# A column roll of 8192 x 8192 floats: the last eighth of the long row pieces issued as DMAs of one row per engine, two in flight on each ring

## The chip, the cores and the metric

The kernel runs on one core of a Trainium2 chip. The metric is the device time in microseconds, as the median of several runs. A core has five instruction streams (TensorE or PE, VectorE or DVE, ScalarE or ACT, GpSimd or POOL, SyncE or SP) and 16 DMA engines. SP, ACT and POOL issue DMAs, and each has a queue of its own to them: in the profile q1 is SP's, q10 is ACT's, q0 is POOL's. The queues of SP and ACT are called rings here. The other core of the pair is idle.

## The reference

```python
def setup_inputs():
    return {"x": np.random.randn(8192, 8192).astype(np.float32), "shift": 100}

def reference(x, shift):
    return np.roll(x, shift, axis=1)
```

Every row moves right by 100 columns, and its last 100 columns come to its front. Nothing is computed: 268 MB are read from the chip's memory and 268 MB are written.

## The kernel before

A row of the output is cut at column `a` = 128, the first multiple of 128 at or after the shift `s` = 100; `g` = a - s = 28.

**The long pieces.** Columns 128 to 8191 of the output are columns 28 to 8091 of the input: 8064 floats or 32,256 bytes of each row, copied from memory to memory without passing through the core. Rows are seen as `"(c e j) w -> j e c w"` with e = 16 and j = 4: row = 64 c + 4 e + j. There are 128 blocks `c` of 64 rows. A DMA (L37) takes one `j`, all 16 values of `e`, and 32 blocks, so its shape is [16, 32, 8064], 16.1 MB, with `e` outermost: each of the 16 DMA engines gets one `e` and copies 32 rows. The loop runs over four `c` ranges and over `j`; `engines[j % 2]` sends even `j` to SP and odd `j` to ACT, so each ring gets eight such DMAs.

**The heads.** The first 128 columns of each row are 512 bytes. POOL reads them into on-chip tiles and writes them again. A row's head is made of the last 100 columns of that row and its first 28 columns. Since the end of one row lies in memory just ahead of the start of the next, three of four heads are read with one piece of 128 floats that runs across the row boundary (`lead`, L67). These pieces are one row apart in what they hold, so DVE copies them into place in the tile `h` (L69 and L72). The fourth is read in two pieces (L68, L71). There are two stages `k` of 4096 rows each, hence ten loads; then eight stores (L76) write the heads.

**Order.** Nothing orders the long pieces against the heads, since their bytes are apart. The framework gives each DMA one of eight semaphores for the hardware queues (shared by SP and ACT) and one of eight for POOL's queue, and a DMA waits until its semaphore's previous user is done. So the fifth to eighth DMA of a ring each wait for the DMA four before them (L37), and POOL's ninth and tenth load (L68 and L71 of the second stage) wait for its first and second. At the end SP waits for all of them.

Of the kernel before, what the change touches and what calls it, by code (L numbers as in the profile page):

```python
# [1 line left out]

# [4 lines left out]


@with_exitstack
def kernel(  # L10
    ctx: ExitStack,
    tc: tile.TileContext,
    x: bass.AP,
    shift: int,
    out: bass.AP,
):
    nc = tc.nc
    n_rows, n_cols = x.shape
    s = shift % n_cols
    a = -(-s // 128) * 128  # L20
    g = a - s
    P = nc.NUM_PARTITIONS
    engines = [nc.sync, nc.scalar]
    n_chunks = 16
    rows = n_rows // n_chunks

    xm = x.rearrange("(c e j) w -> j e c w", e=16, j=4)  # L30
    om = out.rearrange("(c e j) w -> j e c w", e=16, j=4)
    depth = n_rows // 64 // 4
    for c in range(4):
        for j in range(4):
            if a < n_cols:
                cs = slice(c * depth, (c + 1) * depth)
                engines[j % 2].dma_start(out=om[j, :, cs, a:], in_=xm[j, :, cs, g:n_cols - s])  # L37
    if a == 0:
        return


    if a > 512:
        for i in range(n_chunks):
            r = slice(i * rows, (i + 1) * rows)
            nc.gpsimd.dma_start(out=out[r, :s], in_=x[r, n_cols - s:])
            if g > 0:
                nc.gpsimd.dma_start(out=out[r, s:a], in_=x[r, :g])
        return

    Q, J = 4, 8
    n_st = n_rows // (P * Q * J)
    reads = ctx.enter_context(tc.tile_pool(name="reads", bufs=n_st))
    heads = ctx.enter_context(tc.tile_pool(name="heads", bufs=n_st))
    xt = x.rearrange("(k p j q) c -> k q p j c", q=Q, j=J, p=P)
    ot = out.rearrange("(k p j q) c -> k q p j c", q=Q, j=J, p=P)
    tiles = []  # L60
    for k in range(n_st):
        t = reads.tile([P, Q - 1, J, a], x.dtype)
        h = heads.tile([P, Q, J, a], x.dtype)
        for q in range(1, Q):
            lead = bass.AP(tensor=x.tensor, offset=(k * P * J * Q + q) * n_cols - s,
                           ap=[[J * Q * n_cols, P], [Q * n_cols, J], [1, a]])
            nc.gpsimd.dma_start(out=t[:, q - 1], in_=lead)  # L67
        nc.gpsimd.dma_start(out=h[:, Q - 1, :, :s], in_=xt[k, Q - 1, :, :, n_cols - s:])  # L68
        nc.vector.tensor_copy(h[:, :Q - 1, :, :s], t[:, :, :, :s])  # L69
        if g > 0:  # L70
            nc.gpsimd.dma_start(out=h[:, 0, :, s:], in_=xt[k, 0, :, :, :g])  # L71
            nc.vector.tensor_copy(h[:, 1:, :, s:], t[:, :, :, s:])  # L72
        tiles.append(h)
    for k, h in enumerate(tiles):
        for q in range(Q):
            nc.gpsimd.dma_start(out=ot[k, q, :, :, :a], in_=h[:, q])  # L76


# [1 line left out]
_INS = ['x', 'shift']  # L80
_OUTS = [((8192, 8192), 'float32')]

_NUMBERS = {'shift': 100}


# [26 lines left out]
```

## Time and profile before

| what | value |
|---|---|
| median of 8 runs | 831.7 us (827.97 to 832.84) |
| the profiled execution, its own time | 832.84 us |
| its span in the profile | 831.1 us |
| bytes moved by the DMA engines | 272.63 MB in 10784 packets |
| mean rate | 328 GB/s |
| long DMAs on SP and on ACT | 8 each of 16128 KB, median 407.7 and 406.9 us from issue to landing |
| POOL's loads | 10, up to 512 KB, medians 121 to 156 us to landing |
| POOL's stores | 8 of 512 KB, median 187.3 us to landing |
| DVE busy | 3.7 us in 4 copies |

How to read the profile: the span is the time from the first to the last instruction that the profiler saw, and the device time has some 1.7 us around it. The DMA row of part 2 has the mean busy share of the 16 DMA engines in 40 slices of about 20.8 us, in tenths. Part 3 gives each queue's packets, megabytes, and the time of its packets as a share of the time of 16 engines. A DMA-issuing instruction of SP or ACT isn't counted as busy; in the timeline and in the waits its engine is called SPq or ACTq. When windows of time are asked for, each line has the window, its length, busy time and instruction count of DVE and POOL, the clock of PE, the DMA busy share and the rate. A packet is counted in the window in which it starts, so a very short window can show a share above 1.

### The profile page before, as it was taken

The numbers are of one execution on the slowest core, as the hardware profiler recorded it, in microseconds if no ns is written. First come the engines' busy times: TensorE is split into PE (matmuls) and PEld (weight loads), VectorE is DVE, ScalarE is ACT, GpSimd is POOL, SyncE is SP. The second block draws the span as 40 slices with busy tenths as digits, with TensorE's granted clock in tenths as the row PEclk, the third lists the DMA queues.
The fourth block names the chain that finished last, engine by engine and source line by source line (L and its number), as shares of the span: only waits on it lengthen the run. The fifth ranks groups of instructions, "written<-read, shape, count | busy, mean of one in ns | idle before, by whom it ended". The sixth has DMA issues, their size and how long they took to land. (4 is left out here: it accounts for less than half of the span.)

```text
span 831.1 us, 93 instructions
## 1 busy us (share of the span) xinstructions
DVE 3.7 (0%) x4; POOL 16.1 (2%) x22
## 2 busy tenths in 40 slices
DVE  0000000000000000000000000000000000000000
POOL 3000001000010000000000000000000000000000
DMA  9999999999999999999999999999999999999996
GB/s 301 319 342 323 318 335 333 330 339 329 337 328 341 332 338 340 334 341 329 345 325 336 337 332 320 332 324 329 326 323 331 324 329 323 320 334 326 328 332 258
DMA packets 10784, 272.63 MB, mean 328 GB/s; under 512 B 544, under 2 KB 544, under 8 KB 2592
## 3 DMA queue, kind: packets, MB, share of 16 engines
q1 hardware_dynamic: 4224, 132.12, 47.0%
q10 hardware_dynamic: 4224, 132.12, 46.9%
q0 software_dynamic: 2336, 8.39, 4.7%
HBM read 268.44 MB, written 268.44 MB: 646 GB/s over the span
## 5 line engine op out<-in xcount | busy, mean ns | idle before, releaser
L76 POOL DMA_DIRECT2D out_dram<-h x8 | 6.9, 955 | 175.0 <-DMA h<-in_x_dram 148.3
L67 POOL DMA_DIRECT2D t<-in_x_dram x6 | 5.4, 911 | 0.8 <-PEq L107 0.8
L69 DVE COPY h<-t 128x2400 f32<-128x2400 f32 x2 | 2.8, 1411 | 213.6 <-DMA t<-in_x_dram 213.6
L71 POOL DMA_DIRECT2D h<-in_x_dram x2 | 1.8, 882 | 29.3 <-DMA t<-in_x_dram 29.3
L68 POOL DMA_DIRECT2D h<-in_x_dram x2 | 1.8, 883 | 27.0 <-DMA t<-in_x_dram 27.0
L72 DVE COPY h<-t 128x672 f32<-128x672 f32 x2 | 1.0, 504 | 0.0
L93 POOL MEMSET const-float32-0.0<- 128x1 f32 x1 | 0.1, 98 | 0.2 <-issue 0.2
L93 POOL MEMSET const-bfloat16-1.0<- 128x1 bf16 x1 | 0.1, 101 | 0.0
L93 POOL MEMSET const-float32-1.0<- 128x1 f32 x1 | 0.1, 98 | 0.0
L93 POOL MEMSET const-uint8-127<- 128x1 uint8 x1 | 0.1, 98 | 0.0
## 6 DMA issues: line engine op xcount, KB each, us to landing
out_dram<-in_x_dram ACTq DMA_DIRECT2D x8, 16128.0 KB, 406.9
out_dram<-in_x_dram SPq DMA_DIRECT2D x8, 16128.0 KB, 407.7
out_dram<-h POOLq DMA_DIRECT2D x8, 512.0 KB, 187.3
t<-in_x_dram POOLq DMA_DIRECT2D x6, 512.0 KB, 121.1
h<-in_x_dram POOLq DMA_DIRECT2D x2, 400.0 KB, 155.9
h<-in_x_dram POOLq DMA_DIRECT2D x2, 112.0 KB, 149.9
```

Source lines behind the costliest of these rows:

```text
L67: nc.gpsimd.dma_start(out=t[:, q - 1], in_=lead)
L68: nc.gpsimd.dma_start(out=h[:, Q - 1, :, :s], in_=xt[k, Q - 1, :, :, n_cols - s:])
L69: nc.vector.tensor_copy(h[:, :Q - 1, :, :s], t[:, :, :, :s])
L71: nc.gpsimd.dma_start(out=h[:, 0, :, s:], in_=xt[k, 0, :, :, :g])
L72: nc.vector.tensor_copy(h[:, 1:, :, s:], t[:, :, :, s:])
L76: nc.gpsimd.dma_start(out=ot[k, q, :, :, :a], in_=h[:, q])
L93: nc = _bacc.Bacc("TRN2", target_bir_lowering=False, num_devices=1)
```

## The change

- The long pieces of the first 112 of 128 blocks are issued as before, in ranges of 32, 32, 32 and 16 blocks: on each ring six DMAs of [16, 32, 8064] and two of [16, 16, 8064].
- The last 16 blocks are issued one block and one `j` at a time: 32 DMAs per ring, each [16, 8064], one row for each of the 16 DMA engines. Two semaphores per ring (`slots`) alternate: a DMA is issued only when the DMA two before it on the ring has landed on all 16 engines. The first two are issued without a wait, behind the large ones.
- All DMAs and the copies of DVE stand in one critical section (`tc.tile_critical()`), in which the framework adds no waits; all engines meet on entry and on exit. The large DMAs of a ring share one semaphore (`bulk`), and a ring waits for it only after its last issue.
- POOL's ten loads are issued without waits among them. They count on one semaphore per stage (`landed0`, `landed1`), and DVE's first copy of a stage waits for all five loads of that stage. The stores of a stage wait for its copies (`paired`).
- All DMA issues now have the line of the helper `issue`, L47; the critical section is L43, the copies are L93 and L96.

```diff
-    engines = [nc.sync, nc.scalar]
-    n_chunks = 16
-    rows = n_rows // n_chunks
+    rings = (nc.sync, nc.scalar)
...
-    depth = n_rows // 64 // 4
-    for c in range(4):
-        for j in range(4):
-            if a < n_cols:
-                cs = slice(c * depth, (c + 1) * depth)
-                engines[j % 2].dma_start(out=om[j, :, cs, a:], in_=xm[j, :, cs, g:n_cols - s])
...
+    blocks = n_rows // 64
+    whole = blocks * 7 // 8
+    depth = 32
+    window = 2
...
+    with tc.tile_critical():
+        expect = {}
+
+        def issue(eng, sem, o, i):
+            eng.dma_start(out=o, in_=i).then_inc(sem, 16)
+            expect[sem] = expect.get(sem, 0) + 16
...
+        for q, ring in enumerate(rings):
+            bulk = nc.alloc_semaphore(f"bulk{q}")
+            slots = [nc.alloc_semaphore(f"slot{q}_{i}") for i in range(window)]
+            if a < n_cols:
+                for c in range(0, whole, depth):
+                    for j in range(q, 4, 2):
+                        cs = slice(c, min(c + depth, whole))
+                        issue(ring, bulk, om[j, :, cs, a:], xm[j, :, cs, g:n_cols - s])
+                n = 0
+                for c in range(whole, blocks):
+                    for j in range(q, 4, 2):
+                        sem = slots[n % window]
+                        if n >= window:
+                            ring.wait_ge(sem, expect[sem])
+                        issue(ring, sem, om[j, :, c, a:], xm[j, :, c, g:n_cols - s])
+                        n += 1
+            for sem in (bulk, *slots):
+                if sem in expect:
+                    ring.wait_ge(sem, expect[sem])
...
+        for k in range(n_st):
+            t, h = reads[k], heads[k]
+            landed = nc.alloc_semaphore(f"landed{k}")
+            for q in range(1, Q):
...
+                issue(pooled, landed, t[:, q - 1], lead)
+            issue(pooled, landed, h[:, Q - 1, :, :s], xt[k, Q - 1, :, :, n_cols - s:])
+            if g > 0:
+                issue(pooled, landed, h[:, 0, :, s:], xt[k, 0, :, :, :g])
+            nc.vector.wait_ge(landed, expect[landed])
+            nc.vector.tensor_copy(h[:, :Q - 1, :, :s], t[:, :, :, :s]).then_inc(paired, 1)
...
+        for k in range(n_st):
+            pooled.wait_ge(paired, (k + 1) * per)
+            for q in range(Q):
+                issue(pooled, stored, ot[k, q, :, :, :a], heads[k][:, q])
...
+        if stored in expect:
+            pooled.wait_ge(stored, expect[stored])
```

More of the change, by code (lines that the diff above doesn't have):

```diff
@@ L38 @@
[L38 to L45, printed above, removed]
-            if g > 0:
[L47 to L73, printed above, removed]
@@ L74 @@
-    for k, h in enumerate(tiles):
-        for q in range(Q):
-            nc.gpsimd.dma_start(out=ot[k, q, :, :, :a], in_=h[:, q])
+    blocks = n_rows // 64
+    whole = blocks * 7 // 8
+    depth = 32
+    window = 2
+    Q, J = 4, 8
+    narrow = 0 < a <= 512
+    n_st = n_rows // (P * Q * J) if narrow else 0
+    pool = ctx.enter_context(tc.tile_pool(name="heads", bufs=1))
+    reads = [pool.tile([P, Q - 1, J, a], x.dtype, name=f"reads{k}") for k in range(n_st)]
+    heads = [pool.tile([P, Q, J, a], x.dtype, name=f"heads{k}") for k in range(n_st)]
@@ new lines @@
+    with tc.tile_critical():
[6 more added lines that the diff above has]
+            slots = [nc.alloc_semaphore(f"slot{q}_{i}") for i in range(window)]
+            if a < n_cols:
+                for c in range(0, whole, depth):
[13 more added lines that the diff above has]
+                    ring.wait_ge(sem, expect[sem])
+        pooled = nc.gpsimd
+        paired = nc.alloc_semaphore("paired")
+        stored = nc.alloc_semaphore("stored")
+        xt = x.rearrange("(k p j q) c -> k q p j c", q=Q, j=J, p=P)
+        ot = out.rearrange("(k p j q) c -> k q p j c", q=Q, j=J, p=P)
+        n_pair = 0
+        for k in range(n_st):
+            t, h = reads[k], heads[k]
+            landed = nc.alloc_semaphore(f"landed{k}")
+            for q in range(1, Q):
+                lead = bass.AP(tensor=x.tensor, offset=(k * P * J * Q + q) * n_cols - s,
+                               ap=[[J * Q * n_cols, P], [Q * n_cols, J], [1, a]])
+                issue(pooled, landed, t[:, q - 1], lead)
+            issue(pooled, landed, h[:, Q - 1, :, :s], xt[k, Q - 1, :, :, n_cols - s:])
+            if g > 0:
+                issue(pooled, landed, h[:, 0, :, s:], xt[k, 0, :, :, :g])
+            nc.vector.wait_ge(landed, expect[landed])
+            nc.vector.tensor_copy(h[:, :Q - 1, :, :s], t[:, :, :, :s]).then_inc(paired, 1)
+            n_pair += 1
+            if g > 0:
+                nc.vector.tensor_copy(h[:, 1:, :, s:], t[:, :, :, s:]).then_inc(paired, 1)
+                n_pair += 1
+        per = n_pair // n_st if n_st else 0
+        for k in range(n_st):
+            pooled.wait_ge(paired, (k + 1) * per)
+            for q in range(Q):
+                issue(pooled, stored, ot[k, q, :, :, :a], heads[k][:, q])
+        if a > 0 and not narrow:
+            for r in range(0, n_rows, 512):
+                issue(pooled, stored, out[r:r + 512, :s], x[r:r + 512, n_cols - s:])
+                if g > 0:
+                    issue(pooled, stored, out[r:r + 512, s:a], x[r:r + 512, :g])
+        if stored in expect:
+            pooled.wait_ge(stored, expect[stored])
```

## The prediction, made before the changed kernel ran

> **What bounds the kernel now.** I began with the page: parts 1 to 3 say which resource is full, parts 4 to 6 what waits.
>
> ```profile
> span 831.1 us, 93 instructions
> DVE 3.7 (0%) x4; POOL 16.1 (2%) x22
> DMA  9999999999999999999999999999999999999996
> DMA packets 10784, 272.63 MB, mean 328 GB/s; under 512 B 544, under 2 KB 544, under 8 KB 2592
> q1 hardware_dynamic: 4224, 132.12, 47.0%
> q10 hardware_dynamic: 4224, 132.12, 46.9%
> q0 software_dynamic: 2336, 8.39, 4.7%
> ```
>
> No compute engine matters; the 16 DMA engines are busy in 98.6% of their time (47.0 + 46.9 + 4.7). q1 and q10 are the rings of SP and ACT: 4224 packets each are 4096 row pieces and 8 x 16 semaphore writes. So a row piece of 32,256 B is one packet, and each engine moves 256 of them for each ring. At the page's 328 GB/s over 16 engines a row takes 32,256 B / 20.5 GB/s = 1.57 us. Only the last slice of the DMA line is below 9, so I asked for the busy share in small stretches of the end.
>
> ```profile
> 790.00:800.00 10.00, 0.00 (x0) 0.00 (x0) 1.00 0.96 332
> 800.00:810.00 10.00, 0.00 (x0) 0.00 (x0) 1.00 0.91 329
> 810.00:820.00 10.00, 0.00 (x0) 0.00 (x0) 1.00 0.84 313
> 820.00:822.00 2.00, 0.00 (x0) 0.00 (x0) 1.00 0.71 306
> 822.00:824.00 2.00, 0.00 (x0) 0.00 (x0) 1.00 0.67 290
> 824.00:826.00 2.00, 0.00 (x0) 0.00 (x0) 1.00 0.67 290
> 826.00:828.00 2.00, 0.00 (x0) 0.00 (x0) 1.00 0.53 226
> 828.00:829.00 1.00, 0.00 (x0) 0.00 (x0) 1.00 0.23 97
> ```
>
> The last two columns are the share of the 16 engines that is busy and the rate. The landings of the last two DMAs in the trace, 16 increments each, say the same by engine: one engine is done at 777 us, one at 809, four near 820, ten between 827 and 830. The reader should see that **idle engines cost little until about four are idle**: at share 0.96 and 0.91 the rate is still 332 and 329, as with all 16 (326 from 620 to 720 us), at 0.84, a mean over 16 to 11 engines, it is 313. Below 0.75 it falls with the share: 290 / (0.67 x 16) = 27 GB/s is what one engine does by itself, 1.19 us a row. So twelve engines fill what all share (12 x 27 = 324).
>
> That prices the ragged end. 2.32 MB start after 820 us (the DMA view of that stretch); at 328 GB/s they take 7.1 us, and they took 9.2 to 9.8 (the last packet starts at 828.6 and takes 1.2). With 10 us at 313, another 0.5, **the end loses some 2.5 to 3 us**, and 1.2 of it is a last row, which no schedule removes.
>
> The last view is the issues, in the timeline's and the DMA part's lines:
>
> ```profile
> 0.74 507.97 SPq L37 DMA_DIRECT2D out_dram<-in_x_dram  x8
> 0.74 512.39 ACTq L37 DMA_DIRECT2D out_dram<-in_x_dram  x8
> 2.00:2.20 0.20, 0.00 (x0) 0.20 (x1) 1.00 1.88 484
> out_dram<-h POOLq DMA_DIRECT2D x8, 512.0 KB, 187.3
> ```
>
> SP and ACT start at 0.74 us, the first packets between 2.00 and 2.20: 1.3 to 1.5 us from issue to data, take 1.4. The rings are full: a fourth DMA holds its queue 99 us until there is room. POOL's last store is issued at 248 us and lands about 187 later.
>
> **What the Trainium skill says.** All in "DMA: Bandwidth & Descriptors". "Anatomy of one DMA — SWDGE (gpsimd) path" gives a fixed cost of about 2.0 us per DMA, most of it the write receipt. The trace agrees on the sum and not on the place: 1.4 us lie before the first packet and 0.4 between an engine's semaphore packet and the increment that arrives (0.40 us for the engine that ends at 777 us, 0.34 for the last), 1.8 in all. "Why a DMA increments its semaphore by 16 and not by 1" says that the outermost dimension picks the engines, so [16, 8064] uses all 16 with one row each; the 16 increments that the trace has for each [16, 32, 8064] DMA agree. "Queues, rings and completion order" says an engine alternates between rings by packet; the equal 47.0% and 46.9% agree. "Latency and other measured facts" tells of lock-stepped streams at power-of-two row pitches that lose half the rate, from 512 KiB up; here the engines are 4 rows, 128 KiB, apart, and in the first stretch, where all start together, the rate from 10 to 20 us is 327 GB/s: no loss shown.
>
> **The change, part by part.**
>
> Bulk. Of 128 blocks 112 stay in large DMAs: on each ring six of 32 rows per engine and two of 16, where there were eight of 32. The framework's waits on its own semaphores ahead of the fifth to eighth go (four of them, 49.3 us on SP, 16.9 the longest). Worth nothing: at least two whole DMAs, 64 rows x 2 rings x 1.57 = 200 us of work, lie queued then.
>
> The last eighth. 32 DMAs per ring of one row per engine, 33.0 MB in both, 100.7 us at 328 GB/s. It adds 64 DMAs, thus 1024 semaphore packets of 9 ns in the trace, 64 x 9 ns = 0.6 us for an engine; hidden, since an engine has 24% to spare (1.19 against 1.57 us), and 0.6 us if it were not. It adds 30 waits on each ring. Behind a wait stand only further rows of that ring, and who waits for them is the exit. What a wait does is in the round: a slot's row is done on its slowest engine, 0.4 to the increment, under 0.1 for the wait and the issue, 1.4 to data: 1.9 us. In that time the slowest engine still has three rows (one of this ring, two of the other), 3 x 1.57 = 4.7 us, or 3.6 at its lone rate. So **the slowest engine does not run dry**, with 1.7 to 2.8 us in hand; faster ones do, and four may idle for nothing. For an issue under load the trace shows nothing. Bounds of this stage: nothing lost, or 12% (the rate of 290 with ten engines busy), 12 us; a gain of 2% (334 to 335 GB/s between 300 and 500 us against 327 from 450 to 720) if evenly paced engines are kinder to memory, 2 us. I take 1% lost, **+1.0 us**.
>
> The end. Engines now finish within a row or so of each other. The early one idles at the seam instead, from about 7/8 x 777 = 680 us to 726, alone or with few others, for little by the table. Of the 2.5 to 3 us 1.3 to 1.8 can be had; some raggedness stays, so I take **-1.2 us**, between 0 and -3.
>
> The critical section. A handshake over all engines on entry and one on exit. The nearest row is the entry barrier of before, from the first instruction to the first issue 0.74 us. I take **+0.5 us** for both, between 0.2 and 1.5. They are in the open.
>
> POOL and DVE. Ten loads go out back to back, done at about 1.5 + 10 x 0.89 = 10.4 us, where two waited until 35.5 and 65.6; DVE's first copy waits for five loads, not three; stores wait only for the copies. Bytes and packets are the same, 4.7% of the engines wherever they lie. The last stores land near 435 us now, 390 us before the end: nothing, even if they came 100 us later. If they reached past 726 they would take a turn in the rounds, up to 5%, 5 us; I exclude that.
>
> Sum: +1.0 - 1.2 + 0.5 = +0.3 us. The profiled execution took 832.84 us, span 831.1 and 1.7 around it, so 833.1 for it; it lay 1.1 above the median of 831.7. Against the median: **832.0 us**.
>
> **Rivals.**
>
> Slower: the refill becomes the bound. The stage is 16 rounds, each of both slots of both rings, and at full rate a round has 100.7 / 16 = 6.3 us. The trip is 1.9; then a row waits for the other ring's and moves itself, 1.5 + 1.5 us at the median of the packet records, 2.3 + 2.3 at their 99th percentile, and each DMA waits for the slowest of 16: 4.9 to 6.5 us. From 6.3 us on every further tenth costs 1.6 us. An issue that takes 0.5 us longer with busy rings gives rounds of 6.7 and 16 x 0.4 = +6.4: 838 us. For it: the tail of slow rows; no small DMA in the trace. Against it: the mean round is well under 6.3. In the same direction, if engines in step at 128 KiB pitch lose 3% of the stage, 3 us: 835.
>
> Faster: the stage holds its rate or gains, and the end is repaired whole: -2.7 or so, +0.5 for the handshakes, and up to -2 from pacing: 828 to 829.8 us. For it: the rate was higher early. Against it: the most that the end offers is small.
>
> That the change does not do what it says: 32 row DMAs stand on each ring in the built order, so I give this nothing.
>
> **Chances.** Even 0.39, refill or alignment 0.38, gain 0.23. A measurement of this kernel tells about 0.2% (1.7 us) from no change; thus faster 0.23, within 0.39, slower 0.38. The even case by itself holds 830.1 to 833.4. The range 829 to 838 leaves out some 8% below and 12% above, the deeper starvation.
>
> **What would show it.** Packets 10784 + 1024 = 11808 and 1568 under 512 B. SP's waits at the issue line: some 30 of about 3.1 us from about 726 us on. The rate from 730 to 825 us at 322 or more, with share about 0.9; the share falling from over 0.85 to nothing within 4 us at the end. Step by step wrong: share under 0.75 and rate under 315 in that stretch (refill); share near 1 and a low rate (alignment); a rate of 333 or more (pacing); stores beyond 700 us; a first issue later than 1.3 us (handshake). The prediction is wrong if the stage takes under 98 or over 105 us.

## The result, and the profile after

The changed kernel takes 837.39 us (median of 11 runs, 835.0 to 840.16) against 831.84 us for the kernel before (32 runs): a ratio of **1.0067, interval 1.0053 to 1.0082**, 5.6 us slower. The forecast of 832.0, no change, was wrong. The time lies inside the stated range of 829 to 838 only because the range made room for the rival in which the refill becomes the bound (838).

The page of the profiled execution (837.56 us, span 835.8), parts 1 to 3:

```profile
span 835.8 us, 161 instructions
DMA  9999999999999999999999999999999999789897
DMA packets 11808, 272.64 MB, mean 326 GB/s; under 512 B 1568, under 2 KB 1568, under 8 KB 3616
q10 hardware_dynamic: 4736, 132.12, 47.0%
q1 hardware_dynamic: 4736, 132.12, 46.0%
```

The packets are the 11808 expected. The ragged last slice has become a dent six slices wide. In small stretches, and from 735 to 805 us as a whole (window, length, DVE and POOL busy, clock, DMA share, GB/s):

```profile
710.00:720.00 10.00, 0.00 (x0) 0.00 (x0) 1.00 0.89 332
720.00:730.00 10.00, 0.00 (x0) 0.00 (x0) 1.00 0.71 294
730.00:740.00 10.00, 0.00 (x0) 0.00 (x0) 1.00 0.81 287
740.00:750.00 10.00, 0.00 (x0) 0.00 (x0) 1.00 0.86 300
...
735.00:805.00 70.00, 0.00 (x0) 0.00 (x0) 1.00 0.91 313
...
790.00:800.00 10.00, 0.00 (x0) 0.00 (x0) 1.00 0.87 303
800.00:810.00 10.00, 0.00 (x0) 0.00 (x0) 1.00 0.90 310
810.00:820.00 10.00, 0.00 (x0) 0.00 (x0) 1.00 0.95 316
...
830.00:832.00 2.00, 0.00 (x0) 0.00 (x0) 1.00 0.94 290
832.00:834.00 2.00, 0.00 (x0) 0.00 (x0) 1.00 0.00 0
```

Three things are to be seen. At the seam, where the large DMAs end and the row DMAs begin (720 to 750 us), share and rate fall together: against 328 GB/s (34 + 41 + 28) x 10 us / 328 = 3.1 us are lost. In the rounds after it, in which each ring refills its two slots, the rate stays low, 313 GB/s from 735 to 805 us. And the end stops sharply, as intended: share 0.94 and then nothing, where before it ebbed away over 10 us.

SP's waits (what waited, for what: us in total, times, longest), and four issues in the timeline (start, length):

```profile
SPq L47 <- DMA out_dram<-in_x_dram: 277.3, 30, 198.6
SPq L70 <- DMA out_dram<-in_x_dram: 5.6, 1, 5.6
SPq L43 <- POOLq L43: 0.9, 1, 0.9
```

```profile
767.06 0.51 SPq L47 DMA_DIRECT2D out_dram<-in_x_dram  x1
767.24 0.52 ACTq L47 DMA_DIRECT2D out_dram<-in_x_dram  x1
769.45 0.51 SPq L47 DMA_DIRECT2D out_dram<-in_x_dram  x1
769.63 0.52 ACTq L47 DMA_DIRECT2D out_dram<-in_x_dram  x1
```

The 30 waits are the slots' (the first, 198.6 us, is for the large DMAs ahead). The last line of the waits is new: the exit of the critical section waits for POOL. In the timeline **SP and ACT refill in pairs, 0.18 us apart**, 2.4 us from the next pair. Those pairs became the clue. Around the first of them, by microsecond:

```profile
766.00:767.00 1.00, 0.00 (x0) 0.00 (x0) 1.00 0.92 355
767.00:768.00 1.00, 0.00 (x0) 0.00 (x0) 1.00 0.23 97
768.00:769.00 1.00, 0.00 (x0) 0.00 (x0) 1.00 1.60 452
769.00:770.00 1.00, 0.00 (x0) 0.00 (x0) 1.00 0.18 65
```

A row counts in the microsecond in which it starts. From 767 to 768 few rows start, since most engines have done all that they were given; 1.3 us after SP's issue at 767.06 nearly all engines start at once.

### The profile page after: what moved, and what is told of

The parts are those of the page before. It is cut to its first block, busy times and chain, and to the rows that moved or that the text cites. A ratio compares the mean times of both kernels' runs of the same rounds, so it can differ in the third digit from the quotient of the medians.

```text
span 835.8 us, 161 instructions
## 1 busy us (share of the span) xinstructions
DVE 3.7 (0%) x4; POOL 16.1 (2%) x22
## 2 busy tenths in 40 slices
DMA packets 11808, 272.64 MB, mean 326 GB/s; under 512 B 1568, under 2 KB 1568, under 8 KB 3616
## 5 line engine op out<-in xcount | busy, mean ns | idle before, releaser
L47 POOL DMA_DIRECT2D out_dram<-heads x8 | 7.0, 1007 | 234.3 <-DVE heads L96 234.3
L47 POOL DMA_DIRECT2D reads<-in_x_dram x6 | 5.4, 910 | 1.1 <-PEq L140 1.1
L93 DVE COPY heads<-reads 128x2400 f32<-128x2400 f32 x2 | 2.8, 1410 | 244.2 <-DMA heads<-in_x_dram 244.2
L47 POOL DMA_DIRECT2D heads<-in_x_dram x4 | 3.5, 882 | 0.0
L96 DVE COPY heads<-reads 128x672 f32<-128x672 f32 x2 | 1.0, 503 | 0.0
```

The source lines that it names most:

```text
L47: eng.dma_start(out=o, in_=i).then_inc(sem, 16)
L93: nc.vector.tensor_copy(h[:, :Q - 1, :, :s], t[:, :, :, :s]).then_inc(paired, 1)
L96: nc.vector.tensor_copy(h[:, 1:, :, s:], t[:, :, :, s:]).then_inc(paired, 1)
```

## The experiments

The theory I went in with, W: the waits on the slots starve the engines, at the seam and in the rounds. Rivals: S, the 64 small DMAs cost by themselves; H, the critical section costs all. The runs below fell on other chips than the first result, on which the kernel before takes 820.3 to 820.8 us. So each is given as its ratio to the kernel before on its own chip, with the 95% interval; 0.001 is 0.8 us.

| run | rows in flight | ratio | interval |
|---|---|---|---|
| e3: section alone | all large | 1.0013 | 1.0005 to 1.0022 |
| e1: rows without waits | unlimited | 1.0030 | 1.0021 to 1.0040 |
| e4: seam, no rounds | 2 per ring, once | 1.0014 | 1.0002 to 1.0027 |
| e5 | 1 per ring | 1.0602 | 1.0581 to 1.0623 |
| the change, again | 2 per ring | 1.0073 | 1.0045 to 1.0101 |
| e6: last sixteenth | 2 per ring | 1.0038 | 1.0025 to 1.0051 |
| e10 | 3 per ring | 1.0023 | 1.0010 to 1.0035 |
| e2 | 4 per ring | 1.0018 | 1.0005 to 1.0030 |
| e8: DMAs of two rows | 2 x 2 per ring | 1.0016 | 1.0005 to 1.0027 |
| e9: one ring | 4 on SP's ring | 1.0022 | 1.0006 to 1.0038 |
| e7: no section, an eighth | 4 per ring | 0.9994 | 0.9981 to 1.0007 |
| e11: no section, a sixteenth | 4 per ring | 1.0000 | 0.9987 to 1.0012 |

**The critical section alone** (e3).

```diff
-    whole = blocks * 7 // 8
+    whole = blocks
```

> All 128 blocks in large DMAs (eight of 32 rows per ring), all else of the change kept: the critical section, the semaphores, POOL's loads without waits. Theory W: before plus 0.25 us at the start and 1.3 at the end: 833.4 us. Rival S: the same 833.4. Rival H: 837. If POOL's earlier loads do harm, it shows here as a lower rate before 450 us.

Measured 822.11 us against 820.56: 1.0013, with the expected 833.4 / 831.84 = 1.0019 inside the interval, and H falls. The trace shows where it sits: the first row starts at 2.37 us and not 2.17, and from the last row's end to the end of the span it takes 2.5 us and not 1.3. POOL's loads without waits do no harm that shows: the rate from 100 to 300 us is 338 GB/s here, and 338 in e7 too, which keeps POOL's loads as they were before.

**Row DMAs without waits** (e1).

```diff
-                        if n >= window:
-                            ring.wait_ge(sem, expect[sem])
```

> The changed kernel with the 32 row DMAs of each ring issued without any wait among them. Theory W (the wait on the slots starves the engines, at the seam and in the rounds): 833.3 us, that is the kernel before plus some 1.5 us of entry and exit of the critical section; the rate from 730 to 820 us is back at 325 to 330 GB/s and the ragged end is back too. Rival S (64 more small DMAs and their semaphore writes cost by themselves): 836 to 838, rate about 310. Rival H (the critical section costs all of it): 837.

Measured 822.83 against 820.56, 1.0030. More than half of the change's loss is gone, and the rate from 720 to 760 us is 326 to 332. But W's expectation was 833.3 / 831.84 = 1.0018, and against the section alone 0.0017 or 1.4 us stay, with intervals that barely overlap. So S may hold a little; the runs don't settle it, since e2 and e10 have as many small DMAs and show less.

**The seam alone** (e4).

```diff
-                for c in range(whole, blocks):
+                for cs in (slice(whole, whole + 1), slice(whole + 1, blocks)):
...
-                        issue(ring, sem, om[j, :, c, a:], xm[j, :, c, g:n_cols - s])
+                        issue(ring, sem, om[j, :, cs, a:], xm[j, :, cs, g:n_cols - s])
```

> One seam and no rounds: the first two row DMAs of each ring as in the change, then a wait for each, then the rest of the last eighth as two DMAs of 15 rows per engine. Theory W with the loss at the seam (720 to 750 us: 294, 287 and 300 GB/s in the profile of the change, 3 us): 836 us, and a full rate after 745 us. If the rounds hold all of the loss: 833.5. Rivals S and H: 833.5 and 837.

Measured 1.0014, no more than the section alone: my price for the seam fails as a net loss. These stretches of e4 and then of e3 show why:

```profile
710.00:730.00 20.00, 0.00 (x0) 0.00 (x0) 1.00 0.78 300
735.00:805.00 70.00, 0.00 (x0) 0.00 (x0) 1.00 0.99 334
800.00:810.00 10.00, 0.00 (x0) 0.00 (x0) 1.00 0.99 332
```

```profile
710.00:730.00 20.00, 0.00 (x0) 0.00 (x0) 1.00 0.99 326
735.00:805.00 70.00, 0.00 (x0) 0.00 (x0) 1.00 0.92 329
800.00:810.00 10.00, 0.00 (x0) 0.00 (x0) 1.00 0.74 310
```

The dent is there, 26 x 20 / 328 = 1.6 us, but the engines meet at it and stay busy afterwards (share 0.99 for 0.92). From 735 to 805 us that gives 5 x 70 / 328 = 1.1 us back. The spans of these two executions differ by the remaining 0.5 us (820.3 and 819.8), while the median of all runs is no longer for e4 (821.48 against 822.11). **Here evening out the engines moved most of the loss from the end to the seam; it didn't remove it.**

**Two rows in flight, again**, on a chip with the variants:

> The changed kernel as it is, beside the other variants on one chip. Section alone was 1.0013 of the kernel before, four in flight 1.0018, one seam 1.0014. Theory W (the rounds of two are the loss): 1.004 to 1.007, with a rate of about 310 GB/s through the last eighth and 15 or more rows over 2.6 us. Rival C (the first result was that chip's alone): 1.0015 to 1.002, like the variant with four in flight.

Measured 826.01 against 820.76, 1.0073. Rival C falls: the loss isn't one chip's. The trace doesn't agree in each number. From 720 us to the end 11 rows took over 2.6 us (15 in the first trace), and the rate is 324 GB/s where I expected about 310:

```profile
735.00:805.00 70.00, 0.00 (x0) 0.00 (x0) 1.00 0.94 324
```

That execution was a short one (its span is 823.0 us, when the median run would have about 824.3).

**One row in flight** (e5, `window = 1`).

> One row DMA in flight on each ring. Theory W: the trip from the last landing to new data (0.4 to the increment, 0.5 for the issue, 0.8 to the first packet, about 1.8) is now in the open; with a row of 1.2 to 2.0 us on an engine that ran dry, a wait for the other ring's row and the slowest of 16, a row takes some 4.5 us a ring, 32 x 4.5 = 144 us for 101: 40 us longer (ratio 1.05). Rival R (the trip doesn't matter and the loss is that of uneven engines alone): within 5 us of the changed kernel.

Measured 870.68 against 820.76, 50 us more, somewhat over the 40 expected; rival R falls. Its rate:

```profile
735.00:805.00 70.00, 0.00 (x0) 0.00 (x0) 1.00 0.74 224
```

SP issues every 4.66 us in its trace, 32 x 4.66 = 149 us for the stage. This prices the trip. An engine that ran dry gets its row 1.30 us after the issue starts (0.51 of it the issue itself), an increment comes 0.34 us after a row's end, and under 0.1 passes between: 1.7 us, as the prediction had it (1.9).

**Half as many rounds** (e6, `whole = blocks * 15 // 16`).

> Row DMAs, two in flight, for the last sixteenth in place of the last eighth: 8 rounds in place of 16, one seam as before. Theory W: what the changed kernel loses over the section alone is halved: ratio about 1.0035. If the loss lay in the seam: as the changed kernel, 1.005 to 1.0067. If it lay in the end: also as the changed kernel.

Measured 1.0038. Over the section alone the change loses 0.0060, and this 0.0025: roughly in step with the rounds, as W says.

**Three and four rows in flight** (e10 and e2, `window = 3` and `window = 4`).

> Three row DMAs in flight on each ring. One gave 1.060, two 1.0073, four 1.0018. Theory W (six rows in hand, 9 us of work against a trip of 2 us and slow rows of up to 3): 1.002 to 1.003, nearly all of the loss gone. If the loss falls in step with the number in flight: 1.0045.

> Four row DMAs in flight on each ring, not two. Theory W: eight rows per engine cover a slow row of 3 us and the trip of about 2.3 us, and most of the ragged seam of 11 us: 833 us (832 to 834), rate from 740 to 820 us 322 GB/s or more. Rival S: as the changed kernel, 837. Rival H: 837.

Measured 1.0023 and 1.0018. The step is between two and three rows, not in proportion. Their rate from 735 to 805 us is 329 in both, and at the seam (710 to 730) 326 and 335: a third row covers the dent too.

**Two rows in each DMA** (e8).

```diff
-                for c in range(whole, blocks):
+                for c in range(whole, blocks, 2):
...
-                        issue(ring, sem, om[j, :, c, a:], xm[j, :, c, g:n_cols - s])
+                        issue(ring, sem, om[j, :, c:c + 2, a:], xm[j, :, c:c + 2, g:n_cols - s])
```

> Two DMAs in flight on each ring as in the change, but each of two rows per engine (16 DMAs per ring): eight rows in flight in an engine with half the DMAs. Theory W (what counts is the work that an engine has in hand while a slot is refilled): as with four single rows in flight, 1.002. Rival N (the count of DMAs in flight, or the wait itself, is what costs): 1.005 to 1.007.

Measured 1.0016, and 332 GB/s from 735 to 805 us. With two DMAs in flight and a wait for each, the loss is gone: N falls.

**Four in flight, all on one ring** (e9, `window = 4`).

```diff
-                for c in range(whole, blocks):
-                    for j in range(q, 4, 2):
+                for c in range(whole, blocks if q == 0 else whole):
+                    for j in range(4):
```

> The last eighth on SP's ring alone, four row DMAs in flight (64 of them), ACT's ring only with its large ones: four rows in flight in an engine as in the change, without two rings that wait for the same slow row and refill together. Theory W (rows in hand): 1.006 to 1.008. Rival B (the two rings refill in pairs, and this bunching is the loss): 1.003.

Measured 822.17 against 820.34, 1.0022: W, as I had put it, falls here, and rival B holds. An engine has four rows in hand as in the change, and the loss is mostly gone.

```profile
720.00:730.00 10.00, 0.00 (x0) 0.00 (x0) 1.00 0.83 294
735.00:805.00 70.00, 0.00 (x0) 0.00 (x0) 1.00 0.99 332
```

The dent at the seam stays; the rounds run at 332. So two rings of two are worse than one ring of four. The packet records show an order that can account for it. A ring's semaphore write is a packet of its own, of 4 bytes and 9 ns. When both rings have work in an engine, the order there is a row of one ring, a row of the other, then both writes. One engine of the change around 765 us: SP's row ends at 765.50, ACT's row at 766.69, and only then, at 766.68 and 766.69, come the two writes. SP's write is one row late, 1.2 us, and both slots come free together.

Counted from 735 to 805 us, SP rows whose write does not follow within 15 ns: 0 of 720 with one ring; 0 of 240 with one per ring; about 300 of 360 with four per ring; and 23 of 343 in the change. In the change it is the engines that are behind and so have work on both rings. They often decide: of the 28 SP DMAs that land between 735 and 828 us, 15 get their last increment from such a late write. And 17 of ACT's last 28 issues come within 0.25 us of one of SP's. Neither the late write nor the pairs cost anything by themselves: with three and with four per ring nearly all issues come in such pairs, 24 of ACT's 25 after 730 us, and there each engine has enough in hand to bear it.

What the short window does is seen by counting how many of the 16 engines have a row under way. From 735 to 805 us that is never under 12 in e9, e10 and e2. In the change it is under 12 for a tenth of the time (0.05 of it in the second trace) and falls to one, but never to none: **the slowest engine doesn't run dry; the others stand still together and wait for it.**

**Without the section** (e7 and e11): the kernel before with only its cut changed, so that the framework's eight semaphores give four in flight on each ring.

```diff
-    depth = n_rows // 64 // 4
-    for c in range(4):
+    blocks = n_rows // 64
+    whole = blocks * 7 // 8
+    cuts = [*range(0, whole, 32), *range(whole, blocks + 1)]
+    for c0, c1 in zip(cuts, cuts[1:]):
...
-                cs = slice(c * depth, (c + 1) * depth)
+                cs = slice(c0, c1)
```

> The kernel before with only its cut of the long pieces changed: six large and two half DMAs and 32 row DMAs on each ring, with the framework's own eight semaphores and so four in flight on each ring; no critical section, POOL as before. Theory W: the variant with four in flight (1.0018) less the section (0.0013): 1.000 to 1.001, and perhaps 0.999 where the end is repaired. Rival S (small DMAs cost by themselves): 1.002 or more.

> The kernel before with only its cut changed, row DMAs for the last sixteenth, four in flight by the framework's own semaphores, no critical section. With an eighth this was 0.9994. Theory W: the rounds cost little, the end is repaired, less time in rounds: 0.998 to 1.000. If the row DMAs were what helps: 1.000.

(e11 is the same with `15 // 16`.) Measured 0.9994 and 1.0000. Both hold 1.0000 in their intervals: with the section and the short window gone, the row DMAs neither gain nor lose anything that these runs can tell. None of the versions tried is faster than the kernel before beyond its interval.

## Why the prediction was right or wrong

Right: the bound (the shared rate, with four idle engines for little: in e9 it is 332 GB/s with 12 engines or more at work), the packets, a first issue at 0.96 us (under 1.3), an end that stops within a few us, some 30 waits on SP, and that POOL's part doesn't matter. Its last store was in at 475 us, not 435, still 245 us ahead of the seam. One reading was a little off: by the landings three engines end near 820 us and eleven after 825, not four and ten.

Wrong were three terms of the sum, all in one direction.

- **The rounds, +1.0.** Measured: the change against three in flight, 0.0073 - 0.0023 = 0.0050, 4.1 us; against four, 4.5 us. Both intervals together leave some 1.6 to 6.6 us, and a third row's gain at the seam is in it. The trip was priced well, and the conclusion that the slowest engine does not run dry held. The failed step is "faster ones do, and four may idle for nothing", with the count before it, "In that time the slowest engine still has three rows". An engine that is behind has work on both rings, and its first row's write comes only after the other ring's row. By then it has two rows in hand, not three: of the 1.7 to 2.8 us to spare 1.2 or more are gone. And both rings' refills come at once, so that the faster engines, which have done all that they were given, stand still together and not in turn. If twelve engines fill the shared rate, as the prediction worked out, the time under twelve from 735 to 828 us is worth 4.0 us in the first trace of the change (1.3 us in the second, the short execution, from 735 to 816 us). The prediction says that an engine alternates by packet, and did not apply it to the semaphore's packet. The evidence is the counts above and e9. No run changed the order of the writes alone, and the records don't tell whether a write takes a turn or is held until the other ring's row is done.
- **The end, -1.2.** Measured: about nothing, to within 1.2 us or so by the intervals (e4 against e3: 1.0014 and 1.0013), since the seam costs about what the end saves. I let the early engines idle at the seam "for little by the table", though that table itself gives 290 GB/s once five or six are idle, and two rows per ring, 6.3 us of work, don't bridge engines that reach the seam up to 15 us apart (716 to 731 us by the landings of the large DMAs, leaving out the two earliest).
- **The section, +0.5.** Measured: 1.1 us (0.4 to 1.8), inside the bounds given; e3 has POOL's new order in it too. In the trace 0.2 us is the entry and 1.2 the exit, where POOL takes 1.13 us to drain.

The sum in place of +0.3: 4.1 to 4.5, 0 and 1.1, so 5.2 to 5.6 us; the change lost 5.6 on the first chip and 5.3 (826.01 - 820.76) on the other. That is no separate proof, since the first term is taken from the change's own time. The refill rival had the right place and nearly the right time, 838, with another reason: it wanted a longer issue under load. That its price came so close, and with it that the range holds the result, is luck. The issue takes 0.51 us on SP, more than the prediction's "under 0.1 for the wait and the issue", but that lies within the 1.30 us to first data, so the trip didn't grow. The signs named ahead were split: the rate from 730 to 825 us is 310 GB/s, as for the refill (under 315), at a share of 0.91, not under 0.75. A stage of 98 to 105 us decides nothing: counted from the last landing of the large DMAs (731 us) it took 102 us, but at a ragged seam it has no single start.

Alignment (engines in step at 128 KiB) is not seen: with e9's rounds of single rows at 332 GB/s nothing is left for it to explain.

Open: why in most rounds an engine lies 2 to 3 us behind the others, whether it is the same one (the records don't name the engine), the 1.4 us of e1, and why three and four rows in flight, which fill the dent at the seam, are no faster than the section alone (1.0023 and 1.0018 against 1.0013, with intervals that overlap).

## What to carry to other kernels

When DMAs in flight are bounded, count what the slowest engine still has when its completion is written, after the rows of other rings that go ahead of it, and then ask what the faster engines do meanwhile: it is not enough that the slowest one stays busy. Here two rows per ring looked enough and three were needed; four on one ring, or two DMAs of two rows, did as well. Price an idle tail by what the shared rate loses, not by idle engines, and ask what the cure moves to another place. Of the tail's 2.5 to 3 us no version here gained anything that shows, so the critical section's 1.1 us was a plain cost.

## What the runs showed of the hardware that I had not expected

- With both rings full in an engine, a completion's semaphore write came one row of the other ring late, 1.2 us in the example, and both rings refilled 0.2 us apart. With four per ring this met about 300 of 360 rows of SP's ring and none of ACT's.
- Rows in flight per ring, two rings, rows of 32,256 bytes from memory to memory: one costs 6.0% of the whole kernel over its last eighth, two 0.7%, three and four 0.2%, of which 0.1 is the section.
- Rows that start together on engines which had stood still are slow: in the change those that start from 768.3 to 768.6 us took 1.6 to 2.1 us, and the first rows of the kernel before about 2.0 us. The rows that follow at once on the same engines, from 770.1 us on, took 1.2 to 1.4 us, so it is not the number of engines alone; the runs don't show why.
- POOL's drain at the exit of the critical section took 1.13 us, with its DMAs long done.
